# The diagonal of a state-space scan moved into its skip term, and a later place for its transposes

## The chip, the cores and the metric

One core of a Trainium2 chip runs the whole kernel. The metric is the device time of one execution in microseconds (us). Five engines work side by side, each through its own queue in order: TensorE (PE, with its weight loads as PEld) for matmuls and transposes, VectorE (DVE), ScalarE (ACT) and GpSimd (POOL) for work on elements, and SyncE (SP), which here issues all DMA transfers.

## The reference, cut to what matters

One layer of a hybrid backbone: 2048 latent tokens, 1024 wide, and 256 context tokens. A combined input projection feeds a gated spatial MLP and a bidirectional state-space scan (16 heads of 64, two groups of 8 heads, state 128, chunks of 128 tokens); one output projection, a residual, and a SwiGLU FFN follow. The part that the change touches is the scan within a chunk, once per direction:

```python
a_cs = jnp.cumsum(a, axis=2)                     # a = dt * A, per head
xdt = x * dt[..., None]
seg = a_cs[:, :, :, None] - a_cs[:, :, None, :]  # [t, s]
decay = jnp.exp(jnp.where(tri, seg, -jnp.inf))
cb = jnp.einsum('bctgn,bcsgn->bctsg', cm, bm)
y_diag = jnp.einsum('bctsg,bctsge,bcsgep->bctgep', cb, decay, xdt)
...
y = y_f + jnp.flip(y_b, 1)
y = y.astype(h.dtype) + xs * d_skip[:, None]
```

So for each head a chunk has a 128x128 matrix: the product `cb` of the group, times a decay and a step `dt` for each direction. The forward direction holds s <= t, the backward one s >= t. On the diagonal the decay is 1 in both, so it is `cb[t, t] * (dt_f[t] + dt_b[t])`.

## The kernel before

The kernel works in two blocks of 1024 tokens. For each block `xbc` projects and convolves x, B and C of the scan, transposes them to token order and stores records `rec`, one for each chunk of 128 tokens and group of 8 heads: x (512 columns), B (128), C (128) and two masked copies of `cb`, `R_WF` and `R_WB` (128 each). `dt_block` makes the steps `dt_sb`, their running sums `acs` and `nacs` (the backward sums with the sign turned) and stores the sums by rows in `fscr`, so that they can be loaded broadcast over all partitions.

The scan's output is made by `ssd_y`, which goes over 16 chunks and 2 groups, 32 iterations. It is a generator, and so are the projections. `run` takes turns between the main line (`proj_z`, `proj_v`, `proj_u` of block 0, then `out_half` four times) and the side line (`ssd_bwd`, then `ssd_y`), with 2.74 steps of the side line to one of the main line. That sets the order in which instructions are handed over; from it each engine gets a queue that it works off in order. PE's queue thus mixes the projections' matmuls (L228 to L230) with those of the scan.

An iteration of `ssd_y` is, in order: `y_seg` of the next (chunk, group), which makes for each quad of heads a tile `Gt` of four 128x128 matrices (L719 to L731); at group 0 `y_norm` of the chunk before (Newton steps on 128x2 numbers on DVE, then a scaling copy of each group's result on ACT, L778); `y_out` (L744 to L770), with the matmuls for the two carried states (L748, L749), eight matmuls with `Gt` as weights (L751), the state's update, the skip term (L764) and the gate; the load of the record after next; and at group 0 `y_store` of the chunk before, eight PE transposes of the normalised tiles (L785), two copies and two stores into `sscr`, which the second half of the output projection reads.

Nearly all tiles of 128x512 in this part come from one pool, `tma`, with 14 buffers (`NTMA`). A record has 2 buffers (`NREC`), PSUM 4 banks for the projections (`mmp`) and 4 for the rest (`smp`).

Of the kernel before, what the change touches and what calls it, by code (L numbers as in the profile page):

```python
# [7 lines left out]
F32 = mybir.dt.float32  # L8
F32R = mybir.dt.float32r
I32 = mybir.dt.int32  # L10
AF = mybir.ActivationFunctionType
# [30 lines left out]
HID = 2816  # L42
NJ = HID // P
EPS = 1e-6
GELU_C = 0.7978845608028654
GELU_A = 0.044715

# [25 lines left out]
R_X = 0  # L73
R_B = 512
R_C = 640
R_WF = 768
R_WB = 896
R_N = 1024


@with_exitstack
def kernel(ctx: ExitStack, tc: tile.TileContext, xT, ctxp, cc, crow, wad1, wad2, vecs, rows,
# [303 lines left out]
    NT = NCH + NCC  # L386
    dt_sb = cst.tile([P, NT, 32], F32, name="dt_sb")
    acs = cst.tile([P, NT, 32], F32, name="acs")
    nacs = cst.tile([P, NT, 16], F32, name="nacs")
    eac = cst.tile([P, NT, 32], F32, name="eac")  # L390
    ddt = cst.tile([P, NT, 32], F32, name="ddt")
    tot = cst.tile([P, NT, 32], F32, name="tot")
# [2 lines left out]
    def dt_block(c0, stat):  # L395
        nch = sum(n for n, _ in stat) // P
        dfs = []
        for n, xs in stat:
            pd = mmp()
            for k in range(KT):  # L400
                for h in range(2):
                    PE.matmul(pd[:, :n], lhsT=wd2f[:, k * 64:k * 64 + P], rhs=xs[k][h], start=(k == 0 and h == 0), stop=(k == KT - 1 and h == 1))
            df = tmp()
            S.copy(df[0:64, :n], pd[0:64, :n])
            dfs.append((df, n))
        yield
        ps = smp()
        i = 0
        for df, n in dfs:
            for c in range(n // P):  # L410
                PE.matmul(ps[:, i * 32:(i + 1) * 32], lhsT=df[0:64, c * P:(c + 1) * P], rhs=sel, start=True, stop=True)
                i += 1
        w = nch * 32
        r = tma()
        e = tma()
        v3 = lambda t: t[:, :w].rearrange("p (a b) -> p a b", b=32)
        V.tensor_tensor(out=v3(r), in0=v3(ps), in1=row[:, 0:32].rearrange("p (o b) -> p o b", o=1).broadcast_to([P, nch, 32]), op=ALU.add)
        S.activation(e[:, :w], r[:, :w], AF.Abs)
        S.activation(e[:, :w], e[:, :w], AF.Exp, scale=-1.0)
        S.activation(e[:, :w], e[:, :w], AF.Ln, bias=1.0)  # L420
        dt = dt_sb[:, c0:c0 + nch, :]
        V.scalar_tensor_tensor(out=dt, in0=v3(r), scalar=0.0, in1=v3(e), op0=ALU.max, op1=ALU.add)
        a = r
        V.tensor_tensor(out=v3(a), in0=dt, in1=negA.rearrange("p (o b) -> p o b", o=1).broadcast_to([P, nch, 32]), op=ALU.mult)
        f, b = slice(0, 16), slice(16, 32)
        pi, px, pt = smp(), smp(), smp()
        for pp, mf, mb in ((pi, C_LE, C_GE), (px, C_GT, C_LT)):
            PE.matmul(v3(pp)[:, :, f], lhsT=masks[:, mf:mf + P], rhs=v3(a)[:, :, f], start=True, stop=True)
            PE.matmul(v3(pp)[:, :, b], lhsT=masks[:, mb:mb + P], rhs=v3(a)[:, :, b], start=True, stop=True)
        PE.matmul(pt[:, :w], lhsT=ones, rhs=a[:, :w], start=True, stop=True)  # L430
        cs = slice(c0, c0 + nch)
        V.tensor_copy(acs[:, cs, :], v3(pi))
        V.tensor_scalar(out=nacs[:, cs, :], in0=acs[:, cs, 16:32], scalar1=-1.0, scalar2=None, op0=ALU.mult)
        for q in range(2):
            pq = smp()
            c4 = c0 + q * 4
            PE.transpose(out=pq[:, :P], in_=acs[:, c4:c4 + 4, :].rearrange("p a b -> p (a b)"), identity=ident)
            t = tma()
            S.copy(t[:, :P], pq[:, :P])
            DMA.dma_start(fscr[c4 // 4].rearrange("o (r x) -> (o r) x", x=P), t[:, :P])  # L440
        S.activation(eac[:, cs, :], v3(pi), AF.Exp)
        S.activation(ddt[:, cs, :], v3(px), AF.Exp)
        V.tensor_tensor(out=ddt[:, cs, :], in0=ddt[:, cs, :], in1=dt, op=ALU.mult)
        S.activation(tot[:, cs, :], v3(pt), AF.Exp)
# [23 lines left out]
    def xbc(blk, hs, hc, tail):  # L468
# [6 lines left out]
        def finish(ch, oc, os):  # L475
            if oc is not None:
                to_tok(oc, 256, 4, ch)
                yield
            for j in range(2):
                o = os[j]  # L480
                q = tb0 + j
                if ch < 10:
                    to_tok(o, TB, q, ch)
                if ch in (8, 9):
                    bt[j] = o
                if ch >= 10:
                    g = ch - 10
                    DMA.dma_start(rec[q][g][:, :, R_C:R_C + P].rearrange("c p x -> p c x"),
                                  o[:, :TB].rearrange("p (c x) -> p c x", x=P))
                    ps = smp()  # L490
                    for c in range(4):
                        cs = slice(c * P, (c + 1) * P)
                        PE.matmul(ps[:, cs], lhsT=bt[j][:, cs], rhs=o[:, cs], start=True, stop=True)
                    for roff, m in ((R_WF, C_LE), (R_WB, C_GE)):
                        t = tma()
                        V.tensor_tensor(out=t[:, :TB].rearrange("p (c x) -> p c x", x=P), in0=ps.rearrange("p (c x) -> p c x", x=P),
                                        in1=masks[:, m:m + P].rearrange("p (o x) -> p o x", o=1).broadcast_to([P, 4, P]), op=ALU.mult)
                        DMA.dma_start(rec[q][g][:, :, roff:roff + P].rearrange("c p x -> p c x"),
                                      t[:, :TB].rearrange("p (c x) -> p c x", x=P))
                yield  # L500

        def mm_ctx(ch, u, raws, rc):
# [204 lines left out]
    h3 = lambda t: t.rearrange("p (a b) -> p a b", b=HD)  # L707
    hv = lambda ap: bc(ap.rearrange("p (a o) -> p a o", o=1), HD)

    def y_load(rp, c, g):  # L710
        return {"rc": load_rec(rp, c, g, True)}

    def y_seg(st, c, g):
        rc = st["rc"]
        Gt = []
        for q in range(2):
            h0 = g * 8 + q * 4
            fb, bb = tma()[:, :TB], tma()[:, :TB]
            o = ((c % 4) * 32 + h0) * P  # L719
            DMA.dma_start(fb, fscr[c // 4][:, o:o + TB].broadcast_to([P, TB]))  # L720
            DMA.dma_start(bb, fscr[c // 4][:, o + 16 * P:o + 16 * P + TB].broadcast_to([P, TB]))
            A = tma()[:, :TB]
            for e in range(4):
                es = slice(e * P, (e + 1) * P)
                h = h0 + e
                S.activation(bb[:, es], bb[:, es], AF.Identity, bias=nacs[:, c, h:h + 1])
                V.scalar_tensor_tensor(out=fb[:, es], in0=fb[:, es], scalar=acs[:, c, h:h + 1], in1=bb[:, es], op0=ALU.subtract, op1=ALU.min)
                S.activation(A[:, es], rc[:, R_WF:R_WF + P], AF.Copy, scale=dt_sb[:, c, h:h + 1])
                V.scalar_tensor_tensor(out=A[:, es], in0=rc[:, R_WB:R_WB + P], scalar=dt_sb[:, c, 16 + h:17 + h], in1=A[:, es], op0=ALU.mult, op1=ALU.add)
            S.activation(fb, fb, AF.Exp)  # L730
            G.tensor_tensor(out=A, in0=A, in1=fb, op=ALU.mult)  # L731
            Gt.append(A)
            yield
        st["G"] = Gt
        if c < NCH - 1:
            xd = tma()[:, :TB]
            G.tensor_tensor(out=h3(xd), in0=h3(rc[:, R_X:R_X + TB]), in1=hv(ddt[:, c, g * 8:g * 8 + 8]), op=ALU.mult)
            st["xd"] = xd
        hb = tma()[:, :TB]
        DMA.dma_start(hb, hscr[c][:, g * TB:(g + 1) * TB])  # L740
        st["hb"] = hb
        yield

    def y_out(st, c, g, ms):  # L744
# [16 lines left out]
            V.tensor_tensor(out=h, in0=h, in1=pS, op=ALU.add)  # L761
        V.tensor_tensor(out=ya, in0=ya, in1=yb, op=ALU.add)
        V.tensor_tensor(out=ya, in0=ya, in1=py, op=ALU.add)
        G.tensor_tensor(out=h3(yb), in0=h3(rc[:, R_X:R_X + TB]), in1=hv(row[:, 64 + g * 8:64 + g * 8 + 8]), op=ALU.mult)  # L764
        V.tensor_tensor(out=ya, in0=ya, in1=yb, op=ALU.add)
        yield
        zt = tma()[:, :TB]
# [24 lines left out]
    def ssd_y(rp):  # L792
# [6 lines left out]
        for i, (c, g) in enumerate(its):  # L799
            if i + 1 < len(its):  # L800
                yield from y_seg(st[i + 1], *its[i + 1])
            if norm is not None:
                yield from y_norm(*norm[:2])
                norm, store = None, (norm[0], norm[2])
            if g == 0:
                ys, ms = [], sml()[:, :2]
            y = yield from y_out(st.pop(i), c, g, ms)
            ys.append(y)
            if i + 2 < len(its):
                st[i + 2] = y_load(rp, *its[i + 2])  # L810
            if store is not None and g == 0:
                yield from y_store(*store)
                store = None
            if g == 1:
                norm = (ys, ms, c)
# [115 lines left out]

    rp = mix.enter_context(tc.tile_pool(name="recp", bufs=NREC))
    hp = mix.enter_context(tc.tile_pool(name="hp", bufs=1))

    LEAD = 8
    h0 = []
# [352 lines left out]
```

## Time and profile before

| | |
|---|---|
| median of 3 runs | 3008.87 us (3003.96 to 3009.21) |
| profiled execution, its own time | 3005.17 us |
| its span, first to last instruction | 3003.4 us |
| mean granted clock of TensorE | 0.967 |
| busy: PE / PEld | 2818.3 us (94%) / 2252.2 us (75%) |
| busy: DVE / ACT / POOL | 2017.5 us (67%) / 1295.1 us (43%) / 642.9 us (21%) |
| moved by DMA | 515.45 MB, 172 GB/s |

The span is that of one profiled execution; the runs have no profile. A clock of 1.00 is 2.4 GHz. In the order of time: block 1's convolutions (to about 250 us), its projections beside the backward scan's states (to about 500), block 0's convolutions (to about 720), the rest of the backward states (to 790), then `ssd_y` beside block 0's projections and the output projection (to about 1530), the end of the output projection (to about 1640), and the FFN.

### The profile page before, as it was taken

The page shows a single profiled execution, that of the slowest core. Times are in us where ns is not written, and L with a number is a line of the kernel's source. Part 1 is how long each engine was busy: PE and PEld are TensorE (multiplying, and loading weights), DVE is VectorE, ACT ScalarE, POOL GpSimd, SP SyncE. Part 2 cuts the span into 40 slices and gives each one's busy share as a digit, 9 for nine tenths or more (in the row PEclk, how much of TensorE's full clock was granted, in tenths as well). Part 3 has the DMA queues.
Part 4 walks back from the last instruction along what each step waited for, and adds up shares of the span by engine and source line. Part 5 has one row for each costly group of instructions (what it writes and reads, how often), then busy time and mean ns, then how long its engine had stood idle before and what let it go on. Part 6 is the DMA issues. An engine that isn't in the chain of part 4 may idle for free. (4 is left out here: it accounts for less than half of the span.)

```text
span 3003.4 us, 37067 instructions
## 1 busy us (share of the span) xinstructions
PE 2818.3 (94%) x12474; PEld 2252.2 (75%) x12474; DVE 2017.5 (67%) x3412; ACT 1295.1 (43%) x2387; POOL 642.9 (21%) x550
## 2 busy tenths in 40 slices
PE   7999999999999888999898699999999899999997
PEld 3787778878677766777676488888778788888885
DVE  6777966885788878877653755556776644445555
ACT  4444343344355555445442433333554333333443
POOL 3100000110131222223100444445120322221000
PEclk8999999999999999999999699999999999999998
DMA  5322567732755668778644344444766433334764
GB/s 221 97 90 83 190 220 232 257 118 88 240 152 155 209 197 253 239 237 250 197 150 122 106 162 158 158 158 168 257 227 201 150 101 100 102 102 134 235 194 155
DMA packets 289771, 515.45 MB, mean 172 GB/s; under 512 B 28198, under 2 KB 88998, under 8 KB 289580
## 3 DMA queue, kind: packets, MB, share of 16 engines
q1 hardware_dynamic: 289580, 513.08, 53.4%
q8 instruction: 98, 1.61, 0.2%
q14 instruction: 93, 0.76, 0.1%
HBM read 375.60 MB, written 137.38 MB: 171 GB/s over the span
## 5 line engine op out<-in xcount | busy, mean ns | idle before, releaser
L970 DVE TENSOR_TENSOR hl<-w,hl 128x1024 fp32r<-128x1024 f32 x286 | 373.8, 1313 | 313.5 <-ACT hl L969 130.3
L969 ACT CAST hl<-w 128x1024 fp32r<-128x1024 f32 x286 | 299.2, 1051 | 435.9 <-PE mmp L1053 126.7
L228 PE MATMUL mmp<-actt,whi 128*128 128x512 f32 x1120 | 455.5, 407 | 6.2 <-DVE tma L575 6.2
L229 PE MATMUL mmp<-actt,whi 128*128 128x512 f32 x1120 | 445.5, 398 | 0.0
L230 PE MATMUL mmp<-actt,wlo 128*128 128x512 f32 x1120 | 444.2, 397 | 0.0
L1052 PE MATMUL mmp<-hl,hl 128*128 128x512 f32 x704 | 277.7, 394 | 37.1 <-ACT hl L969 32.4
L1053 PE MATMUL mmp<-hl,hl 128*128 128x512 f32 x704 | 276.9, 393 | 2.4 <-DVE hl L970 2.4
L1054 PE MATMUL mmp<-hl,hl 128*128 128x512 f32 x704 | 276.7, 393 | 0.0
L228 PEld LDWEIGHTS mmp<-actt,whi 128*128 128x128 f32 x1120 | 214.7, 192 | 55.4 <-DVE tma L575 7.5
L229 PEld LDWEIGHTS mmp<-actt,whi 128*128 128x128 f32 x1120 | 214.5, 191 | 48.1 <-issue 5.3
L230 PEld LDWEIGHTS mmp<-actt,wlo 128*128 128x128 f32 x1120 | 214.5, 192 | 47.6 <-issue 1.7
L228 PE MATMUL mmp<-whi,actt 128*128 128x512 f32 x512 | 212.1, 414 | 0.0
L1052 PE MATMUL smp<-hl,hl 128*128 128x512 f32 x528 | 209.1, 396 | 1.7 <-ACT hl L969 1.6
L1053 PE MATMUL smp<-hl,hl 128*128 128x512 f32 x528 | 207.5, 393 | 0.0
L1054 PE MATMUL smp<-hl,hl 128*128 128x512 f32 x528 | 207.3, 393 | 0.1
L230 PE MATMUL mmp<-whi,actt 128*128 128x512 f32 x512 | 206.9, 404 | 0.0
L229 PE MATMUL mmp<-wlo,actt 128*128 128x512 f32 x512 | 206.3, 403 | 0.0
L1052 PEld LDWEIGHTS mmp<-hl,hl 128*128 128x128 f32 x704 | 133.7, 190 | 67.6 <-ACT hl L969 34.8
L976 DVE TENSOR_TENSOR t<-smp,t 128x512 f32<-128x512 f32 x88 | 60.5, 687 | 180.5 <-PE smp L1054 105.9
L450 DVE SCALAR_TENSOR_TENSOR tma<-xin,cw,tma 128x512 f32<-128x512 f32 x192 | 144.3, 751 | 21.8 <-ACT tma L448 16.2
L1053 PEld LDWEIGHTS mmp<-hl,hl 128*128 128x128 f32 x704 | 133.9, 190 | 31.2 <-DVE hl L970 3.5
L731 POOL TENSOR_TENSOR tma<-tma 128x512 f32<-128x512 f32 x64 | 88.9, 1389 | 319.8 <-ACT tma L730 223.0
(256 smaller groups left out, 5816.5 us busy)
## 6 DMA issues: line engine op xcount, KB each, us to landing
w<-in_wall_dram SPq DMA_DIRECT2D x110, 512.0 KB, 4.0
ws<-in_wall_dram SPq DMA_DIRECT2D x104, 512.0 KB, 4.2
ascr<-t SPq DMA_DIRECT2D x154, 256.0 KB, 4.1
w<-ascr SPq DMA_DIRECT2D x154, 256.0 KB, 2.7
tma<-fscr SPq DMA_DIRECT2D x128, 256.0 KB, 5.5
w<-wscr SPq DMA_DIRECT2D x88, 256.0 KB, 3.5
w<-in_wall_dram SPq DMA_DIRECT2D x66, 256.0 KB, 4.0
rec<-tma SPq DMA_DIRECT2D x64, 256.0 KB, 2.6
```

What stands on the lines that cost most here:

```text
L228: PE.matmul(ps, lhsT=lh, rhs=rh, start=(i == 0), stop=False)
L229: PE.matmul(ps, lhsT=lh, rhs=rl, start=False, stop=False)
L230: PE.matmul(ps, lhsT=ll, rhs=rh, start=False, stop=(i == n - 1))
L450: V.scalar_tensor_tensor(out=acc[:, :n], in0=raw[:, j:j + n], scalar=cw[:, ch, j:j + 1], in1=acc[:, :n], op0=ALU.mult, op1=ALU.add)
L731: G.tensor_tensor(out=A, in0=A, in1=fb, op=ALU.mult)
L969: S.copy(hi, x)
L970: eng.tensor_tensor(out=lo, in0=x, in1=hi.bitcast(F32), op=ALU.subtract)
L976: eng.tensor_tensor(out=o, in0=a, in1=b, op=ALU.add)
L1052: PE.matmul(ps, lhsT=hi[:, ms_], rhs=t[:, 0, :], start=first and k == 0, stop=False, skip_group_check=not first)
L1053: PE.matmul(ps, lhsT=hi[:, ms_], rhs=t[:, 1, :], start=False, stop=False, skip_group_check=not first)
L1054: PE.matmul(ps, lhsT=lo[:, ms_], rhs=t[:, 0, :], start=False, stop=k == 3, skip_group_check=not first)
```

## The change

Four edits come together.

1. `y_seg`: in place of one exponential of the smaller of the two directions' differences and a weight that is made of `R_WF` and `R_WB`, there is one exponential for each direction. The row of running sums gets a mask added (0 inside the strict triangle, -1e30 outside, tiles `cut`), on GpSimd for the forward and on DVE for the backward direction; the exponential's bias is `ln(dt) - acs`, so that it has the step in it. The two are added and multiplied with the unmasked product `cb`.
2. The diagonal, which the strict masks leave out, goes into the weight of the skip term: `dskip = d_skip + cb[t, t] * (dt_f + dt_b)`, per token and head.
3. `xbc` stores `cb` once and unmasked, and reads its diagonal with four products with the identity per group and 512 tokens, each with a sum over the row (`accum_out`).
4. `ssd_y`: `y_store` of the chunk before stands at group 1 in place of group 0.

```diff
-R_WF = 768
-R_WB = 896
-R_N = 1024
+R_CB = 768
+R_N = 896
...
-    nacs = cst.tile([P, NT, 16], F32, name="nacs")
+    nacs = cst.tile([P, NT, 32], F32, name="nacs")
+    dskip = cst.tile([P, NCH, 16], F32, name="dskip")
+    cbd = cst.tile([P, NCH, 2], F32, name="cbd")
...
-        V.tensor_scalar(out=nacs[:, cs, :], in0=acs[:, cs, 16:32], scalar1=-1.0, scalar2=None, op0=ALU.mult)
+        V.tensor_scalar(out=v3(e), in0=dt, scalar1=TINY, scalar2=None, op0=ALU.max)
+        S.activation(e[:, :w], e[:, :w], AF.Ln)
+        V.tensor_tensor(out=nacs[:, cs, :], in0=v3(e), in1=acs[:, cs, :], op=ALU.subtract)
+        c8 = slice(c0, c0 + 8)
+        V.tensor_tensor(out=dskip[:, c8, :], in0=dt_sb[:, c8, 0:16], in1=dt_sb[:, c8, 16:32], op=ALU.add)
+        d4 = dskip[:, c8, :].rearrange("p a (g h) -> p a g h", g=2)
+        V.tensor_tensor(out=d4, in0=d4, in1=bc(cbd[:, c8, :].rearrange("p a (g o) -> p a g o", o=1), 8), op=ALU.mult)
+        V.tensor_tensor(out=dskip[:, c8, :], in0=dskip[:, c8, :], in1=row[:, 64:80].rearrange("p (o h) -> p o h", o=1).broadcast_to([P, 8, 16]), op=ALU.add)
...
-                    for roff, m in ((R_WF, C_LE), (R_WB, C_GE)):
-                        t = tma()
-                        V.tensor_tensor(out=t[:, :TB].rearrange("p (c x) -> p c x", x=P), in0=ps.rearrange("p (c x) -> p c x", x=P),
-                                        in1=masks[:, m:m + P].rearrange("p (o x) -> p o x", o=1).broadcast_to([P, 4, P]), op=ALU.mult)
-                        DMA.dma_start(rec[q][g][:, :, roff:roff + P].rearrange("c p x -> p c x"),
-                                      t[:, :TB].rearrange("p (c x) -> p c x", x=P))
+                    t = tma()
+                    S.copy(t[:, :TB], ps)
+                    dg = tma()[:, :P]
+                    for c in range(4):
+                        cs = slice(c * P, (c + 1) * P)
+                        V.scalar_tensor_tensor(out=dg, in0=ps[:, cs], scalar=1.0, in1=ident, op0=ALU.mult, op1=ALU.mult,
+                                               accum_out=cbd[:, q * 4 + c, g:g + 1])
+                    DMA.dma_start(rec[q][g][:, :, R_CB:R_CB + P].rearrange("c p x -> p c x"),
+                                  t[:, :TB].rearrange("p (c x) -> p c x", x=P))
...
-            A = tma()[:, :TB]
-            for e in range(4):
-                es = slice(e * P, (e + 1) * P)
-                h = h0 + e
-                S.activation(bb[:, es], bb[:, es], AF.Identity, bias=nacs[:, c, h:h + 1])
-                V.scalar_tensor_tensor(out=fb[:, es], in0=fb[:, es], scalar=acs[:, c, h:h + 1], in1=bb[:, es], op0=ALU.subtract, op1=ALU.min)
-                S.activation(A[:, es], rc[:, R_WF:R_WF + P], AF.Copy, scale=dt_sb[:, c, h:h + 1])
-                V.scalar_tensor_tensor(out=A[:, es], in0=rc[:, R_WB:R_WB + P], scalar=dt_sb[:, c, 16 + h:17 + h], in1=A[:, es], op0=ALU.mult, op1=ALU.add)
-            S.activation(fb, fb, AF.Exp)
-            G.tensor_tensor(out=A, in0=A, in1=fb, op=ALU.mult)
-            Gt.append(A)
+            for x, o, eng in ((fb, 0, G), (bb, 16, V)):
+                x3 = x.rearrange("p (e t) -> p e t", t=P)
+                eng.tensor_tensor(out=x3, in0=x3, in1=cuts[0][:, o // 16:o // 16 + 1, :].broadcast_to([P, 4, P]), op=ALU.add)
+                for e in range(4):
+                    es = slice(e * P, (e + 1) * P)
+                    S.activation(x[:, es], x[:, es], AF.Exp, bias=nacs[:, c, o + h0 + e:o + h0 + e + 1])
+            V.tensor_tensor(out=fb, in0=fb, in1=bb, op=ALU.add)
+            f3 = fb.rearrange("p (e t) -> p e t", t=P)
+            V.tensor_tensor(out=f3, in0=f3, in1=rc[:, R_CB:R_CB + P].rearrange("p (o t) -> p o t", o=1).broadcast_to([P, 4, P]), op=ALU.mult)
+            Gt.append(fb)
...
-        G.tensor_tensor(out=h3(yb), in0=h3(rc[:, R_X:R_X + TB]), in1=hv(row[:, 64 + g * 8:64 + g * 8 + 8]), op=ALU.mult)
+        G.tensor_tensor(out=h3(yb), in0=h3(rc[:, R_X:R_X + TB]), in1=hv(dskip[:, c, g * 8:g * 8 + 8]), op=ALU.mult)
...
-            if store is not None and g == 0:
+            if store is not None and g == 1:
```

The tiles `cut` are made once, ahead of the scan, by two small DVE operations.

## Rows read from the trace of the kernel before

**Rows 1.** Busy time by stretch; convolutions of block 0, then the scan's stage.
```profile
core 0: us, PE busy (x) PEld busy (x) DVE busy (x) ACT busy (x) POOL busy (x), PEclk, DMA share, GB/s
...
530.00:720.00 190.00, 186.68 (x865) 155.37 (x864) 156.02 (x244) 82.23 (x126) 28.39 (x55) 0.99 0.51 165
800.00:1560.00 760.00, 688.94 (x3094) 539.90 (x3093) 603.75 (x1401) 402.52 (x1019) 189.87 (x154) 0.95 0.68 207
```

**Rows 2.** Waits of PE, 800 to 1560 us: total, times, longest (us).
```profile
PE smp L785 <- ACT tma L778: 37.2, 8, 8.7
PE smp L751 <- POOL tma L731: 5.0, 3, 2.1
...
PE mmp L228 <- DVE tma L575: 4.7, 2, 2.5
...
PE smp L785 <- DVE tma L754: 2.9, 1, 2.9
PE smp L785 <- DVE tma L755: 2.8, 1, 2.8
```

**Rows 3.** Timeline of PE, 1099.5 to 1112 us: start, duration, instruction, [idle before].
```profile
1106.23 1.97 PE L785 MATMUL smp<-ident,tma 128*128 128x128 f32 x8 [5.76 <-ACT tma L778]
```

**Rows 4.** Timeline of ACT and DVE ahead of the same wait.
```profile
1087.21 0.62 ACT L770 ACTIVATE tma<-tma 128x512 f32<-128x512 f32 x1
...
1092.32 0.17 DVE L775 TENSOR_SCALAR sml<-sml 128x2 f32<-128x2 f32 x1
...
1105.26 0.16 DVE L241 SCALAR_TENSOR_TENSOR sml<-sml 128x2 f32<-128x2 f32 x1
```

**Rows 5.** Eight stretches of half clock behind waits; columns as in rows 1.
```profile
898.99:901.90 2.91, 2.91 (x11) 2.63 (x12) 2.71 (x11) 2.75 (x6) 0.00 (x0) 0.50 0.05 15
...
sum 33.72, PE 33.71 PEld 27.44 DVE 26.44 ACT 16.39 POOL 10.82; mean PE 4.21 PEld 3.43 DVE 3.31 ACT 2.05 POOL 1.35
```

**Rows 6.** Line 748: duration (ns) min/median/max, first and last start (us).
```profile
L748 PE MATMUL smp<-h,rec_sb x64: 590/591/1061, 797.7 to 1510.0; 128*128 128x512 f32 x64
```

**Rows 7.** Groups by line, 785 to 1520 us: busy us, mean ns, idle before.
```profile
L729 DVE SCALAR_TENSOR_TENSOR tma<-rec_sb,dt_sb,tma 128x128 f32<-128x128 f32 x256 | 94.4, 403 | 12.1 <-ACT tma L728 11.9
L727 DVE SCALAR_TENSOR_TENSOR tma<-tma,acs 128x128 f32<-128x128 f32 x256 | 92.6, 399 | 54.5 <-ACT tma L726 53.5 <-DMA tma<-fscr 0.5
L731 POOL TENSOR_TENSOR tma<-tma 128x512 f32<-128x512 f32 x64 | 88.9, 1389 | 319.8 <-ACT tma L730 223.0 <-DVE sml L239 14.7 <-DMA xin<-gmscr 11.7
L726 ACT ACTIVATE tma<-tma,nacs 128x128 f32<-128x128 f32 x256 | 83.9, 390 | 127.4 <-DMA tma<-fscr 125.2 <-DMA ws<-in_wall_dram 1.1 <-issue 0.7
L728 ACT ACTIVATE tma<-rec_sb,dt_sb 128x128 f32<-128x128 f32 x256 | 83.9, 389 | 22.1 <-DMA rec_sb<-rec 22.0
L730 ACT ACTIVATE tma<-tma 128x512 f32<-128x512 f32 x64 | 40.0, 625 | 27.8 <-DVE tma L727 24.5 <-issue 2.3 <-POOL tma L731 0.6
L764 POOL TENSOR_TENSOR tma<-rec_sb,row 128x512 f32<-128x512 f32 x32 | 36.8, 1149 | 69.9 <-issue 20.9 <-DVE tma L762 15.8 <-DVE sml L240 11.4
...
L762 DVE TENSOR_TENSOR tma<-tma 128x512 f32<-128x512 f32 x32 | 25.6, 801 | 0.2
L765 DVE TENSOR_TENSOR tma<-tma 128x512 f32<-128x512 f32 x32 | 24.1, 754 | 9.9 <-POOL tma L764 9.9
```

**Rows 8.** Groups by line, whole span; columns as in rows 7.
```profile
L973 DVE TENSOR_TENSOR t<-t,t 128x512 f32<-128x512 f32 x104 | 95.9, 940 | 1.8
...
L496 DVE TENSOR_TENSOR tma<-smp,masks 128x512 f32<-128x512 f32 x16 | 10.3, 683 | 0.0
...
L186 DVE DVE_READ_ACCUMULATOR tma<-tma 128x1 f32 x64 | 5.3, 82 | 0.0
```

**Rows 9.** Timeline of POOL and DVE near 1087 us.
```profile
1087.04 1.05 POOL L737 TENSOR_TENSOR tma<-rec_sb,ddt 128x512 f32<-128x512 f32 x1 [2.88 <-DMA rec_sb<-rec]
...
1087.34 0.89 DVE L729 SCALAR_TENSOR_TENSOR tma<-rec_sb,dt_sb,tma 128x128 f32<-128x128 f32 x1 [0.24 <-ACT tma L728]
```

**Rows 10.** Waits of SP's queue, 800 to 1520 us: total, times, longest (us).
```profile
SPq L211 <- DVE tma L727: 18.0, 3, 7.6
...
SPq L847 <- POOL tma L731: 10.6, 5, 3.2
```

More of the change, by code (lines that the diff above doesn't have):

```diff
@@ L44 @@
 EPS = 1e-6
+TINY = 1e-37
+BIG = 1e30
 GELU_C = 0.7978845608028654
@@ L708 @@
     hv = lambda ap: bc(ap.rearrange("p (a o) -> p a o", o=1), HD)
+    cuts = []
     def y_load(rp, c, g):
@@ L933 @@
     hp = mix.enter_context(tc.tile_pool(name="hp", bufs=1))
+    cut = hp.tile([P, 2, P], F32, name="cut")
+    for i, m in enumerate((C_LT, C_GT)):
+        V.tensor_scalar(out=cut[:, i, :], in0=masks[:, m:m + P], scalar1=BIG, scalar2=-BIG, op0=ALU.mult, op1=ALU.add)
+    cuts.append(cut)
     LEAD = 8
```

## The prediction

> **What bounds the kernel now.** I first read the busy time by stage, to see where TensorE (PE), the engine that carries the matmuls, isn't full. In 800 to 1560 us, where the output scan runs beside the projections of block 0 and the output projection, PE is busy 688.94 of 760 us at a mean granted clock of 0.95; VectorE (DVE) is busy 603.75, ScalarE (ACT) 402.52, GpSimd (POOL) 189.87 [rows 1]. The reader is to see two losses on one engine there: 760 - 688.94 = 71.1 us idle, and a clock that isn't whole. In 530 to 720 us, where the convolution blocks are edited, PE is busy 186.68 of 190 at 0.99: nothing to win there, and little to lose.
>
> Second, PE's waits in the scan's stage [rows 2]. One of them stands out: the transposes of `y_store` (L785) wait for the normalising copies of `y_norm` (L778), 37.2 us in 8 waits, longest 8.7. Two more waits of L785, 2.9 and 2.8, are on L754 and L755, which free a PSUM bank. Behind these come L751 on POOL's product L731 (5.0) and projections on L575 (4.7).
>
> Third, one such wait in order of time. PE reaches the transposes and stands for 5.76 us until 1106.23 [rows 3]. The last sum of squares that the norm needs is started at 1087.21 on ACT, the norm's first DVE operation at 1092.32, its last at 1105.26 [rows 4]. So the norm's chain of small operations takes 13 us on a DVE that is 79% busy in this stage (603.75 / 760), and the transposes are asked for before it ends. They wait for the order of the work, not for a lack of throughput.
>
> Fourth, the clock after these waits. In the eight stretches behind the larger ones PE works at a granted clock of 0.50, which is 1.2 in place of 2.4 GHz, for 33.71 us in all [rows 5]; at 1.00 that work would take half, so they cost another 16.9 us. Before each of these stretches PE had been idle in such a wait.
>
> **The change, part by part.**
>
> *Transposes half an iteration (one half of a chunk's two) later.* The 64 matmuls of L748, two for each (chunk, group), run from 797.7 to 1510.0 [rows 6]: 31 intervals of 23.0 us. The transposes of chunk c move behind the next group's `y_out`, so they come one such interval later, for 15 of 16 chunks; the last has nothing to move behind. PE came at most 8.7 us too early, and now comes about 23 us later: some 14 us to spare. What goes: the 37.2 us. Of the 2.9 + 2.8 for the PSUM bank I take half, since those depend on `y_out`, behind which the transposes still stand. Sum: -40 us idle. Clock: with 40 of 42.9 us of the waits gone, I take 15 of the 16.9 us. Bounds: nothing if the norm falls as far back as the transposes (below), and 42.9 + 16.9 = 59.8 if all goes. What moves with it: per chunk eight transposes, two ACT copies (L787), two stores of 256 KB on SP's queue, behind the `rec` load of the next group. Their reader, the second half of the output projection, comes much later for all chunks but the last two; the last chunk's store keeps its place.
>
> *The segment part, 64 times.* On DVE, L727 (92.6 us) and L729 (94.4) go: 187.0. Three 128x512 `tensor_tensor` come in for each: 192. The nearest rows are L762 (801 ns) and L765 (754), both of SBUF alone [rows 7]; I take 0.75, so 144. From below the cheapest row of a 128x512 `tensor_tensor` at hand, L496 with 683, gives 131; from above L973's 940 ns [rows 8] gives 180. DVE gains 43, between 7 and 56. On ACT, L726 (83.9), L728 (83.9) and L730 (40.0) go: 207.8. Eight 128x128 exponentials with a per-partition bias come in; L726 has that shape and a bias operand, 83.9 / 256 = 0.328 us each, so 512 x 0.328 = 168. An exponential costs no more than an identity as far as rows go (L730's 625 ns for four times the width is less per element). ACT gains 40. On POOL, L731 (88.9) goes, and an add with a repeated operand comes in 64 times: between L764's 1149 ns (also a repeated operand) and L731's 1389, so 74 to 89. From landing to the finished `Gt` the chain is about as long as before: POOL add 1.3, eight exponentials 2.6, two DVE operations 1.5, so 5.4 us; before it is about 8 x 0.328 + 0.63 + 1.39 = 4.6. L751 has waited for `Gt` 5.0 us in all [rows 2]; I add 4.
>
> None of the 43 or 40 us counts as such, since PE sets the end. What they can buy is the rest of the waits on DVE, 4.7 on L575 and part of the 5.0. I take 3 us.
>
> *The two adds.* GpSimd and DVE now each add a mask to a tile when the two broadcast loads land, at the same time. The trace shows what such company costs: L729 took 0.89 us at 1087.34, beside L737 on POOL from 1087.04, against a mean of 403 ns [rows 7, 9]. The Trainium skill ("GPSIMD Engine Reference", section "8. Key points") says that GpSimd shares its SBUF interfaces with VectorE and contends with DVE instructions that have two SBUF inputs. All three new DVE operations are of that kind, but so were L727 and L729. By the rule at its worst, all three at 940 ns, DVE would gain 7 us in place of 43; by the rows of this stage it gains 43. This decides how much lateness comes back, not whether the transposes wait, and is in the second rival.
>
> *In the convolution blocks.* 16 masked products L496 at 683 ns (10.9 us of DVE) become 32 `scalar_tensor_tensor` of 128x128 with an accumulator read: 403 ns (L729) + 82 (the read after L186) [rows 7, 8] = 15.5 us; 8 PSUM copies on ACT, at most L730's 625 ns each, 5 us; 8 stores fewer. `dt_block` gets a logarithm and a few small DVE operations, under 1 us each, twice. DVE is 156.02 of 190 us busy there [rows 1], PE waits for none of it, and the free time of both engines covers it: 0. If that cover is gone, its whole price is about 4.6 + 5 + 6 = 16 us of two engines, most of it in parallel; I keep +5 as the upper bound. `rec` is an eighth narrower (896 of 1024 columns) to load: no wait on it, so 0.
>
> *What takes the place of the stalls.* Idle time removed from PE brings it earlier to its next dependent instruction. L751 and the PSUM bank that L575 frees are next; both stand at 5 us [rows 2]. I put back 4 us, between 0 and half the gain (30).
>
> Sum: -40 - 15 + 4 - 3 + 4 = -50 us. The profiled execution's own time is 3005.17 us, 3.7 below the median of the runs shown: 3005.2 - 50 = 2955. In runs I expect 2956.
>
> **The rivals.**
>
> *All of it and more* (0.12). The transposes never wait, and DVE's 43 us also end the waits on L751 and L575. -59.8 - 9.7, with 5 us of the clock that is lost around the smaller waits: 2930. For it: DVE is named in three of the four other waits in [rows 2]. Against: POOL and the loads are as late as before.
>
> *Half comes back* (0.18). The norm is late because DVE is full. If the adds beside POOL cost DVE its gain, or if PE's new pace makes `y_out`'s operands late, L751 or L748 wait in place of L785: half of the 59.8 is lost, and 3 us go on the clock around the new waits: 3005 - 30 + 3 = 2978. For it: the slack of `Gt` is shorter by the one us above, and now ends on DVE's queue, behind everything queued there. Against: only 5 us of such waits now.
>
> *No change* (0.06). The norm's operations stand in DVE's queue where they fall due; if they fall due for the transposes, they move back with them, and PE waits as long, one interval later: 3005. Against: the norm's place in the program stays, ahead of `y_out`.
>
> *Slower: tiles are held too long* (0.08). The 14 tiles of the pool `tma` serve everything. Two normalised tiles are held some 23 us longer per chunk, and `fb` now lives until L751 in place of L731; only `A` goes. SP's queue is in order and already waits for such tiles to come free: a weight load (L211) stood 18.0 us behind tiles of L727, an `x2scr` load (L847) 10.6 behind L731 [rows 10]. If weights come later than the three units they are loaded ahead, PE waits at L228. A wait like the one at 1106 costs 5.76 and some 2 of clock; in each of 15 chunks that is 116, less the gain of 50: 3070. It decides from about 7 of 15 chunks on. Against: no wait of PE on weights stands in [rows 2], and `A` was the longest-held tile of a segment.
>
> **How the numbers follow.** The likeliest case (0.56) gives 2956, its own range 2940 to 2972. A difference under 0.2%, 6 us, can't be told from none. Faster: 0.56 + 0.12 + 0.18 = 0.86; same 0.06; slower 0.08. The range takes in the second rival's price and most of the first's: 2927 to 2988.
>
> **What would show it.** Right: L785's waits on L778 nearly gone in PE's list; fewer stretches at half clock between 800 and 1560; that stage some 50 us shorter and the rest of the kernel, above all the FFN, of the same length; DVE's busy time there about 43 us lower and ACT's 40. Wrong: L785 still waiting for L778's successor; new waits of L751 on the last DVE product above 15 us; the new DVE operations well over 0.8 us beside POOL; PE waiting at L228 for weights while SP's queue waits for a tile.

## The result, and the profile after

The changed kernel takes 3031.13 us (median of 5 runs, 3023.9 to 3038.75) against 3008.87 (3003.96 to 3011.82): a ratio of 1.0066, with a 95% interval of 1.0047 to 1.0086. It is slower, by some 20 us; forecast were 50 us less.

Two marks in time say where. They are the first matmul of the scan's output (L748 before, L762 after) and the last update of the residual in the output projection (L848, L862), from the views of those lines:

| profiled execution | first scan matmul | last residual update | from one to the other | span |
|---|---|---|---|---|
| before | 797.7 | 1638.6 | 840.9 | 3003.4 |
| after | 803.7 | 1656.8 | 853.1 | 3024.1 |

So in these two executions 6 us were lost ahead of the scan, 12 between the marks (the scan and the output projection beside and behind it), and 2.5 behind them. The scan's stage with the columns of [rows 1], after:

```profile
800.00:1560.00 760.00, 682.09 (x3041) 534.33 (x3041) 565.16 (x1078) 359.25 (x956) 203.71 (x155) 0.94 0.67 203
```

DVE has 39 us less to do there and ACT 43, as forecast, and PE is idle for 77.9 us in place of 71.1. PE's waits in the same stretch (line 799 is 785 of before, 763 is 749, 768 and 769 are 754 and 755, 775 is 761, 626 and 648 are 613 and 635 of the token mixing):

```profile
PE smp L763 <- DMA tma<-hscr: 21.2, 4, 8.3
PE smp L799 <- DVE tma L768: 16.7, 4, 7.7
PE smp L626 <- DVE xin L648: 15.9, 5, 5.2
PE smp L799 <- DVE tma L769: 9.6, 3, 4.5
PE smp L765 <- DVE h L775: 4.9, 2, 4.8
PE smp L799 <- DVE h L775: 4.8, 3, 3.7
```

The wait on the norm's copies, 37.2 us in [rows 2], is gone altogether. In its place stand the load of the carried backward state `hscr` (21.2), the PSUM banks that the transposes write to (L768, L769, L775: 31.1 us), and more of the token mixing (15.9), which waited 4.9 us before:

```profile
PE smp L613 <- DVE xin L635: 4.9, 2, 4.4
```

The segment's new operations, as in [rows 7]:

```profile
L742 ACT ACTIVATE tma<-tma,nacs 128x128 f32<-128x128 f32 x512 | 160.8, 389 | 180.0 <-POOL tma L739 149.9 <-DVE tma L739 28.1 <-ACT tma L784 0.8
L739 POOL TENSOR_TENSOR tma<-tma,cut 128x512 f32<-128x512 f32 x64 | 90.9, 1420 | 259.9 <-DMA tma<-fscr 201.4 <-issue 14.1 <-DVE actt L845 14.0
...
L739 DVE TENSOR_TENSOR tma<-tma,cut 128x512 f32<-128x512 f32 x64 | 55.6, 872 | 96.5 <-DMA tma<-fscr 96.3
L743 DVE TENSOR_TENSOR tma<-tma 128x512 f32<-128x512 f32 x64 | 53.8, 841 | 16.4 <-ACT tma L742 12.0 <-POOL h L774 2.0 <-issue 1.2
L745 DVE TENSOR_TENSOR tma<-tma,rec_sb 128x512 f32<-128x512 f32 x64 | 45.0, 703 | 0.4
```

The reader is to look at the idle times behind the second bar. POOL stands 201 us and DVE 96 for the broadcast loads, and ACT 150 us for POOL's add.

One of the new waits in order of time, first PE, then DVE ahead of it:

```profile
1310.06 1.12 PE L799 MATMUL smp<-ident,tma 128*128 128x128 f32 x4 [7.67 <-DVE tma L768]
```
```profile
1301.08 6.46 DVE L845 SCALAR_TENSOR_TENSOR actt<-xin,actt 128x512 fp32r<-128x512 f32 x6
1307.46 1.28 DVE L739 TENSOR_TENSOR tma<-tma,cut 128x512 f32<-128x512 f32 x2
1308.67 0.74 DVE L862 SCALAR_TENSOR_TENSOR tma<-mmp,m_sb,tma 128x512 f32<-128x512 f32 x1
1309.33 0.67 DVE L768 TENSOR_TENSOR tma<-smp,eac 128x512 f32<-128x512 f32 x1
```

The transposes' data have been ready for some 38 us (the norm's copies of that chunk start at 1271.22), but the bank is read (L768) only when DVE's queue comes to it, behind the main line's splitting (L845).

### The profile page after: what moved, and what is told of

Its sections match the earlier page's. It is cut to its first block, busy times and chain, and to the rows that moved or that the text cites. A ratio compares the mean times of both kernels' runs of the same rounds, so it can differ in the third digit from the quotient of the medians.

```text
span 3024.1 us, 36720 instructions
## 1 busy us (share of the span) xinstructions
PE 2822.3 (93%) x12474; PEld 2255.7 (75%) x12474; DVE 1984.0 (66%) x3150; ACT 1262.9 (42%) x2333; POOL 652.5 (22%) x550
## 5 line engine op out<-in xcount | busy, mean ns | idle before, releaser
L742 ACT ACTIVATE tma<-tma,nacs 128x128 f32<-128x128 f32 x512 | 160.8, 389 | 180.0 <-POOL tma L739 149.9
L1070 PEld LDWEIGHTS mmp<-hl,hl 128*128 128x128 f32 x704 | 134.0, 190 | 70.4 <-ACT hl L987 36.4
L994 POOL TENSOR_TENSOR w<-w 128x512 f32<-128x512 f32 x44 | 59.7, 1358 | 451.5 <-DVE hl L988 304.1
```

The source lines that it names most:

```text
L742: S.activation(x[:, es], x[:, es], AF.Exp, bias=nacs[:, c, o + h0 + e:o + h0 + e + 1])
L1070: PE.matmul(ps, lhsT=hi[:, ms_], rhs=t[:, 0, :], start=first and k == 0, stop=False, skip_group_check=not first)
```

## The experiments

Ratios are to the kernel before, run on the same chip; the changed kernel's is 1.0066.

| run | edit | median, us | ratio | 95% interval |
|---|---|---|---|---|
| e1 | changed, transposes at group 0 | 3016.1 | 1.0048 | 1.0032 to 1.0064 |
| e2 | before, transposes at group 1 | 3015.08 | 1.0044 | 1.0030 to 1.0058 |
| e4 | changed, transposes into `mmp` | 3021.39 | 1.0065 | 1.0050 to 1.0080 |
| e5 | changed, diagonal from SBUF | 3027.62 | 1.0079 | 1.0059 to 1.0099 |
| e6 | changed, both adds on POOL | 3047.34 | 1.0141 | 1.0121 to 1.0161 |
| e6b | e6, transposes at group 0 | 3047.79 | 1.0142 | 1.0123 to 1.0160 |
| e7 | changed, loads of both quads first | 3026.57 | 1.0065 | 1.0042 to 1.0089 |
| e8 | changed, record load in POOL's queue | 3027.7 | 1.0076 | 1.0061 to 1.0091 |
| e9 | changed, one Newton step | 3010.1 | 1.0016 | 1.0007 to 1.0026 |
| e10 | changed, no broadcast loads | 2938.21 | 0.9776 | 0.9761 to 0.9790 |
| e11 | changed, 13 tiles | 3020.98 | 1.0055 | 1.0040 to 1.0070 |
| e12 | changed, both adds on DVE | 2995.04 | 0.9970 | 0.9956 to 0.9983 |
| e13 | e12, transposes at group 0 | 3000.19 | 0.9979 | 0.9967 to 0.9992 |
| e14 | e12, loads one `y_out` earlier | 3000.08 | 0.9982 | 0.9968 to 0.9995 |
| e15 | before, L731 on DVE | 2993.46 | 0.9962 | 0.9947 to 0.9977 |
| e16 | e10, with the loads, unread | 2980.57 | 0.9914 | 0.9891 to 0.9938 |
| e17 | e15, L764 on DVE too | 2992.49 | 0.9962 | 0.9949 to 0.9976 |
| e18 | e13, skip product on DVE too | 2977.45 | 0.9914 | 0.9892 to 0.9936 |

### The change in two halves (e1, e2)

```diff
-            if store is not None and g == 1:
+            if store is not None and g == 0:
```

e1 makes this edit to the changed kernel, e2 the reverse of it to the kernel before.

> The changed kernel with the transposes back at group 0. Theory A (the later place is to blame: it puts the transposes behind matmuls that hold all four PSUM banks, and keeps two tiles longer): the waits on VectorE's reads of PSUM (26 us in the changed kernel) and on the hscr load (21) fall to a few us, the waits on the norm's copies come back in part (20 to 40 us); 3000 to 3015 us. Theory B (the segment's new operations are to blame, the later place helps): slower than the changed kernel, 3050 or more.

> The kernel before with the transposes at group 1 and nothing else. Theory A: 3010 to 3030 us, with waits of the transposes on VectorE's reads of PSUM in place of those on the norm's copies. Theory B: 2955 to 2975, since the 40 us of waits go and nothing takes their place.

Each half alone costs 13 to 14 us, and the two together 20. Theory A was right on e2, whose waits are those of the changed kernel, with the segment of before:

```profile
PE smp L785 <- DVE tma L754: 19.5, 3, 8.9
PE smp L749 <- DMA tma<-hscr: 19.0, 4, 8.1
PE smp L613 <- DVE xin L635: 12.0, 4, 4.4
```

But the segment is no gain either: in e1 the waits on the norm are back (33.7 us), and the time is a little above what A had allowed. The marks of their profiled executions put the two losses in different places. From first scan matmul to last residual update e2 takes 847.6 us (799.5 to 1647.1), 6.7 more than the kernel before (the rest of its loss is 1.8 ahead and 4.6 behind, where the profiles of all runs spread over 6 us); e1 takes 841.9 (804.7 to 1646.6), only 1.0 more, and lost 7.0 ahead of the scan. There are two causes to look for.

### What the transposes wait for (e4, e5, e11)

```diff
 def y_store(ys, c):
...
-            ps = smp()
+            ps = mmp()
```

> The changed kernel, but the transposes write to the PSUM banks of the projections (mmp) in place of those that the scan's matmuls hold. If the bank is what the transposes wait for: their waits on lines 768, 769 and 775 (31 us) go, and with the clock that comes back 25 to 40 us are won, 2990 to 3005. If the bank is not the cause, or the projections now wait for theirs: 3025 to 3040.

```diff
-                        V.scalar_tensor_tensor(out=dg, in0=ps[:, cs], scalar=1.0, ...
+                        V.scalar_tensor_tensor(out=dg, in0=t[:, cs], scalar=1.0, ...
```

> The changed kernel, but the four small products for the diagonal read the copy in SBUF and not PSUM, so that the bank is free once ScalarE has copied it. If the 4 us stall at 611 us in the convolution blocks comes from the bank: it goes, with some 2 us of clock, and the time is 5 to 8 us lower, about 3024. If not: 3031 as it is.

```diff
-NTMA = 14
+NTMA = 13
```

> The changed kernel with 13 tiles in the pool tma in place of 14. Theory E (tiles that are held longer are what the change pays for): 15 us or more slower, 3038 or more, with longer waits on the hscr load. Theory P: within 6 us of the changed kernel.

e4 takes the transposes' wait on the scan's banks away, and the time doesn't move: now the projections wait for theirs, which an update behind in the same DVE queue frees.

```profile
PE mmp L229 <- DVE tma L862: 24.5, 10, 5.4
```

So the banks seem only to name the place where PE meets DVE's queue. e5 wins nothing: a stall at 610 us stands in it too (3.7 us on L464), and one of 3.3 us stands there in the kernel before (L462 on L454). e11 rules out the pool of tiles: one tile fewer costs nothing, so the tiles that are held longer are not what the change pays for, as the prediction's rival had it.

### Where the adds run, and the loads (e6, e6b, e7, e8)

```diff
-            for x, o, eng in ((fb, 0, G), (bb, 16, V)):
+            for x, o, eng in ((fb, 0, G), (bb, 16, G)):
```

> The changed kernel with both mask adds on GpSimd. Theory C (VectorE's queue, in order, stands 96 us for the broadcast loads in front of its add on line 739, and so reads PSUM later: 14.7 us after the matmul in place of 11.6; the transposes and projections wait for those banks): the idle time on line 739 goes from VectorE, the transposes' waits on lines 768 and 769 (26 us) halve, 2990 to 3010 us. Theory D (the loads come late whoever waits for them, since SP's queue and the tile pool are the limit): 3020 to 3035, GpSimd stands in place of VectorE and the finished weights come later.

> The same with the transposes back at group 0. If the later place is a loss even where VectorE's queue is free (theory A): 2990 to 3005, faster than with the adds alone. If the later place pays once VectorE is free: 15 us or more slower than with the adds alone, since the waits on the norm's copies (34 us) are back.

```diff
-        for q in range(2):
-            ...loads of fb and bb, then the adds
+        for q in range(2):
+            ...loads of fb and bb
+            qs.append((h0, fb, bb))
+        for h0, fb, bb in qs:
```

> The changed kernel, with the four broadcast loads of a (chunk, group) issued together ahead of its first quad, so that the second quad's land earlier. Theories C and D both: the idle time before line 739 falls by a third or more, 3005 to 3020. If instead the pool of 14 tiles is the limit (theory E): two tiles more are held, the hscr load comes later, and the time is 3030 or more.

```diff
-        DMA.dma_start(rc[:, :w], rec[ci // 4][g][ci % 4][:, :w])
+        (G if full else DMA).dma_start(rc[:, :w], rec[ci // 4][g][ci % 4][:, :w])
```

> The changed kernel, with the scan's record loads issued from GpSimd's queue, where the product that frees the record's buffer runs, in place of SP's. SP's queue stands 81 us for that product. Theory D: the loads behind it come earlier, the waits on hscr (21 us) and on the broadcasts fall, 3000 to 3015. Theory C alone: VectorE stands as before, 3022 to 3032.

Theory C is not borne out: in e6 DVE has no mask add that stands for the loads, and yet the kernel is 0.75% slower than the changed one. DVE still stands, though, now 88 us for ACT, which stands 193 for POOL's add:

```profile
L739 POOL TENSOR_TENSOR tma<-tma,cut 128x512 f32<-128x512 f32 x128 | 178.3, 1405 | 230.5 <-DMA tma<-fscr 195.5 <-DMA tma<-hscr 9.2 <-DMA x2scr<-tma 5.2
L742 ACT ACTIVATE tma<-tma,nacs 128x128 f32<-128x128 f32 x512 | 163.3, 390 | 192.9 <-POOL tma L739 192.7
L743 DVE TENSOR_TENSOR tma<-tma 128x512 f32<-128x512 f32 x64 | 57.0, 891 | 104.8 <-ACT tma L742 88.3 <-POOL tma L739 6.9 <-issue 6.4
```

The place of the transposes makes no difference there (e6b). Loads issued earlier within a segment (e7) and a record load that SP's queue does not stand for (e8) make none either. SP's queue stands 81 us for L778 (the skip product, L764 of before) in the changed kernel; without that, PE's wait on `hscr` is 4.8 us in e8 and the time is the same, so those 81 us are not what costs.

### The pace (e9, e10, e12)

```diff
 def newton(ms, w):
...
-        for _ in range(3):
+        for _ in range(1):
```

> The changed kernel with one Newton step in place of three (the numbers are less exact): 12 small VectorE operations fewer per chunk and norm, some 39 us of VectorE's work in the scan's stage. In the changed kernel the transposes come 25 us behind the norm's copies, so the norm's own length can't matter. Theory P (VectorE's queue sets the pace of this stage, and a stall that is taken from TensorE comes back as a wait on VectorE): 20 to 40 us less, 2985 to 3005. Theory L (late loads set it): 3018 to 3028.

```diff
-            DMA.dma_start(fb, fscr[c // 4][:, o:o + TB].broadcast_to([P, TB]))
-            DMA.dma_start(bb, fscr[c // 4][:, o + 16 * P:o + 16 * P + TB].broadcast_to([P, TB]))
...
-                eng.tensor_tensor(out=x3, in0=x3, in1=cuts[0][...], op=ALU.add)
+                eng.tensor_tensor(out=x3, in0=cuts[0][...], in1=cuts[0][...], op=ALU.add)
...
-                    S.activation(x[:, es], x[:, es], AF.Exp, bias=nacs[...])
+                    S.activation(x[:, es], x[:, es], AF.Exp, bias=dt_sb[...])
```

> The changed kernel without the 128 broadcast loads of the running sums: the two mask adds read the mask twice, and the exponentials take another bias, so the scan's weights are not the reference's; all other instructions stand. Theory L: 40 us or more less, under 2985, since GpSimd's 205 us and VectorE's 96 us of waiting on these loads go. Theory P: 5 to 25 less, 3000 to 3018, only by what VectorE no longer waits.

```diff
-            for x, o, eng in ((fb, 0, G), (bb, 16, V)):
+            for x, o, eng in ((fb, 0, V), (bb, 16, V)):
```

> The changed kernel with both mask adds on VectorE. With both on GpSimd it was 20 us slower. If GpSimd's slower add, late in the chain from the load to the finished weights, is what costs: 10 to 20 us less, 3003 to 3015. Theory P: VectorE has 45 to 55 us more work, so 20 us or more slower, 3042 or more.

e9 wins 0.5%, 15 us of the 20 to 40 that theory P had: less work in DVE's queue shortens the stage even where nothing on the path needs that work. e10 wins 2.9%, and PE is nearly full, with DVE busier than before:

```profile
800.00:1560.00 760.00, 738.75 (x3423) 585.94 (x3422) 610.77 (x1126) 383.10 (x990) 201.78 (x154) 0.99 0.55 174
```

So P's main claim falls: 610.77 us of DVE work in 760 go along with a PE at 97%. e12 goes against P as well. DVE gets 37 us more for the add (92.3 in place of 55.6), and the kernel is 0.96% faster than the changed one, 0.3% faster than the one before:

```profile
L739 DVE TENSOR_TENSOR tma<-tma,cut 128x512 f32<-128x512 f32 x128 | 92.3, 728 | 82.3 <-DMA tma<-fscr 78.9 <-PE smp L799 2.4 <-DMA ws<-in_wall_dram 0.7
```

128, 64 and no mask adds on POOL are 1.0141, 1.0066 and 0.9970: some 23 and 29 us for each 64.

### What of the loads costs, and whose the gain of e12 is (e13 to e16)

e13 is e12 with the edit of e1. e14 issues the four loads of a (chunk, group) one `y_out` earlier; e15 and e16 are

```diff
-            G.tensor_tensor(out=A, in0=A, in1=fb, op=ALU.mult)
+            V.tensor_tensor(out=A, in0=A, in1=fb, op=ALU.mult)
```
```diff
+            fl, bl = tma()[:, :TB], tma()[:, :TB]
+            DMA.dma_start(fl, fscr[c // 4][:, o:o + TB].broadcast_to([P, TB]))
+            DMA.dma_start(bl, fscr[c // 4][:, o + 16 * P:o + 16 * P + TB].broadcast_to([P, TB]))
```

the first in the kernel before, the second in e10.

> Both mask adds on VectorE (e12, 0.3% under the kernel before), with the transposes back at group 0. If the later place is a loss in itself, as in the pairs so far (+7 with the old segment, +6 to 12 with the new one): 2985 to 2992. If it pays once the chain is shorter: 3002 or more.

> As e12, with the four broadcast loads of a (chunk, group) issued a whole y_out earlier, so that they have landed when the mask adds come up; four tiles more are held at a time. If the landing is what the stage waits for and the pool has room (13 tiles cost nothing): 2955 to 2985. If the pool binds now: 3000 or more.

> The kernel before, with the product of decay and weight (line 731) on VectorE in place of GpSimd. If leaving GpSimd alone is what gave the 28 us: 20 us or more faster than before, 2975 to 2985, though VectorE has 44 us more work. If VectorE's work counts there: 3010 to 3040.

> As the kernel without broadcast loads, but the 128 loads are issued again, into tiles that nothing reads (the weights are not the reference's). If the wait for their landing is what costs: 2935 to 2960. If their traffic and their place in SP's queue cost: 3000 to 3025.

e15 says that the gain of e12 is not the change's: the kernel before has it too, 0.4%, once its product leaves POOL. e16 lies between its two forecasts: with the loads back but unread, 1.5% under the changed kernel (46 us), 1.4% above the one without loads. So the loads cost in two ways, about half each: by the work that waits for their landing, and by being issued at all. The second half is not traffic alone. e16 takes two tiles more per quad from the pool, PE waits 21.9 us for `hscr` in it (0.7 in e10), and POOL's adds stand 42.9 us for tiles that such a load still fills:

```profile
L740 POOL TENSOR_TENSOR tma<-cut 128x512 f32<-128x512 f32 x62 | 76.8, 1242 | 172.7 <-DMA sscr<-tma 43.7 <-DMA tma<-fscr 42.9 <-ACT tma L785 22.8
```

e13 and e12 can't be told apart, so the later place of the transposes, a loss of 13 us in e2, is neither gain nor loss here. e14's waits on the broadcasts fall to 49.7 us and its time doesn't: its transposes wait 19.9 us for the bank.

### The same step once more (e17, e18)

```diff
-        G.tensor_tensor(out=h3(yb), in0=h3(rc[:, R_X:R_X + TB]), ...
+        V.tensor_tensor(out=h3(yb), in0=h3(rc[:, R_X:R_X + TB]), ...
```

> The kernel before with lines 731 and 764 on VectorE. If any product on GpSimd in a chain costs here: another 8 to 15 us, 2975 to 2987, and SP's wait on line 764 (86 us) shrinks. If VectorE's load counts by now (22 us more): 2995 or more.

> The changed kernel with both mask adds and the skip product on VectorE and the transposes at group 0. By the same reasons 2982 to 2992, or 3002 or more.

On the kernel before (e17) it gives nothing more; on the change with both adds on DVE and the transposes at group 0 (e18) another 0.65%. e18 is the fastest that computes the reference, 0.9914 of the kernel before, some 26 us less:

```profile
800.00:1560.00 760.00, 710.55 (x3263) 557.06 (x3262) 601.27 (x1205) 381.66 (x982) 73.97 (x59) 0.98 0.69 210
```

PE is idle for 49.4 us there, in place of 71.1 and 77.9, and the transposes' waits on the norm's copies are still 27.5 us of that. e17 and e18 are also like for like: both have the transposes at group 0, and the segment's chain and the skip product off POOL. Between them the change of segment and diagonal is worth 15 us, and their intervals do not overlap. With the skip product on POOL (e15, e13) it is worth nothing; why that product decides it stays open.

## Why the prediction was wrong

**The step that failed** is "What takes the place of the stalls", with 4 us put back. The runs put back all of the gain and more: e2, which is that edit alone, wins no 55 us but loses 13. For the 37.2 us that went, there came 31.1 us on the transposes' banks (6.5 before), 21.2 on `hscr` (none before) and 15.9 on the token mixing (4.9 before). That last wait was as long as the two that the step named as next, and was passed over. The sentence under it that misled is "They wait for the order of the work, not for a lack of throughput". PE's wait on the norm was where PE met a side line that was late everywhere. Without it PE runs further ahead: from the start of L748 to that of L754, the first read of its PSUM, the mean over the 32 (chunk, group) pairs is 11.6 us before, 13.8 in e2, 14.7 in the changed kernel (L762 to L768), and 10.5 in e1. By group one sees the wait's part in it. It stood between the `y_out` of group 0 and that of group 1, and held PE back for the latter: the mean of group 1 is 9.1 us before and 14.9 in e2, that of group 0 14.1 and 12.8. PE then waits for the banks, the `hscr` load and the mixing. That PE runs ahead once the wait is gone, and that the waits move from one place to the next, is shown by e2 and e4; that the queues of the side line, waiting for one another, set the pace is the reading that fits e9, e10, e12 and e16, and no single run shows it by itself.

**Right in mechanism:** L785's wait on L778 is gone (37.2 to 0). The norm's copies of one chunk start at 1059.55, its transposes at 1081.52, 22 us or about an interval later. The stage's clock did not come back (0.94 in place of 0.95): new waits as long as the old ones stand in it, and behind the one that ends at 1310.06 the granted clock is 0.50 until 1313, where it was 1.00 ahead of it.

**The wait for the bank** was seen (2.9 and 2.8 us) and mis-sized: with the norm out of the way it is 31.1. In the kernel before the longer wait seems to have hidden it, for the transposes stood behind a `y_out` there too.

**The segment's costs** came out: DVE's three operations are 154.4 us (forecast 144, 131 to 180), ACT's exponentials 160.8 (168), POOL's add 90.9 (74 to 89, so just above). None of it was worth time while POOL stood in the chain. "From landing to the finished `Gt` the chain is about as long as before" counted durations and left out the queues: ACT stands 150 us behind POOL's add, and POOL 201 for the load. In the kernel before POOL had its operation at the end of that chain (L731, 64 times), and e15 shows that it cost there as well.

**The rule on GpSimd and VectorE.** DVE's add takes 872 ns where POOL adds beside it and 728 in e12 where it doesn't, L743 841 and 717. The Trainium skill ("GPSIMD Engine Reference", section "8. Key points") names such contention, and these rows agree. Over 64 of each that is some 17 us of DVE's time, yet e12, where the adds and the two operations behind them (L743, L745) take 182.6 us of DVE in place of 154.4, was faster. So the price looks more like the chain's than the contention's; no run changes one without the other.

**The rivals.** "Half comes back" had the mechanism, PE's new pace meeting late operands, and half the size. The slower rival had the sign and a load that PE waits for, but its cause was the tile pool, which e11 excludes, and the load was `hscr`, not the weights.

**Ahead of the scan** the forecast was 0 to +5; 6 us were lost. e1 and e5, with the same edits there, start the scan at 804.7 and 802.2, e2 without them at 799.5. The place is behind block 1's convolutions, where its projections run beside the backward states: PE is busy for 199.5 us of 275 to 485 in the changed kernel, 199.4 in e1 and 199.7 in e13, against 203.5 before, 201.9 in e2 and 204.0 in e15. Which of the small edits does it stays open, as e5 excludes only the read from PSUM. In block 0's convolutions "PE waits for none of it" was a misreading: PE waits 3.3 us for DVE there before (L462 on L454) and 4.8 after.

**Open besides:** why loads that are issued earlier (e7, e14) win nothing while loads that nothing reads (e16) do, and whether e18 with the later transposes would be faster still; neither was run further.

## What to carry to other kernels

A long wait on a full engine is worth its length only if what the engine meets next is early; before counting it, ask how late the other queues are at the next meeting point, and look for a second wait that the first one hides. Move an edit of the order alone (e2) apart from the edits of the work, since either may spoil the other. Where a chain of load, add, exponential and product feeds the bound engine, count the time that each queue stands for the one ahead, not only durations, and try the slowest engine's link on another one, even on a busier engine.

## What was not expected of the hardware

Moving 64 adds of 128x512 from GpSimd (1.42 us each) to VectorE (0.73) won 29 us with VectorE busy for 589 of 760 us. And the broadcast loads, 128 of 256 KB, cost about 41 us even when nothing read them (e16 against e10); the wait for the tiles that they fill is in that.
